# A hybrid decoder layer on one core: the output projection's turned rows copied out of PSUM first, four summed pairs in its second block, and weight buffers dealt by kind

## The chip, the core and the metric

The kernel runs on one core of one Trainium2 chip. The metric is the device time of one execution in microseconds (us). The median of three runs of the kernel before is 1082.09 us (1081.95 to 1083.99).

The engines are named as in the profile: PE is the matrix engine (PEld its weight loads), DVE the vector engine, ACT the scalar engine, POOL GpSimd, SP the engine that issues most of the loads.

## The reference

One decoder layer on 256 tokens of width 2048, in float32:

```python
u = rmsnorm(h, ln1_w)
lru_x, lru_g, q, k, v, ret_g = split(u @ w_in)        # six parts of 1024
y_lru = rg_lru(conv4(lru_x)) * gelu(lru_g)            # group A
y_ret = groupnorm(retention(rope(q), rope(k), v)) * silu(ret_g)   # group B, 8 heads
h = h + concat(y_lru, y_ret) @ w_out                  # 2048 x 2048
u = rmsnorm(h, ln2_w)
h = h + (silu(u @ w_gate) * (u @ w_up)) @ w_down      # D_FF = 5632
return rmsnorm(h, final_norm_w)
```

## The kernel before

**Split products.** Every float32 operand of a large product is cut into a high and a low part of a shorter matmul format: `split` (L122 to L124) is an ACT cast into `wh` (`ah`, `sh`, `bh`, `t4h`) and a DVE subtraction into `wl` (`al`, `sl`, `bl`, `t4l`). A product is then three matmuls, high by high, high by low and low by high (`three`, L683 to L685, tile `c`). Loads of weights bring 128x1024 raw tiles (512 KB) from SP's queue; each is cast by ACT, subtracted by DVE, and read by PE.

**Stages.** First v, the eight tiles of lru_x, k and q, v and the gates, each with its scan or its retention; then the output projection in two blocks of 1024 columns (block 0 and block 1, here "output blocks"), then the FFN's blocks 2 to 12, the down projection (two blocks) and the final norm. On the time axis, output block 0's steps run from about 294 to 343 us and block 1's to about 388.

**Pairs and steps.** A block's contraction of 2048 is cut into eight pairs of 256. A *plain* pair takes the eight half products of `EIGHT`, 24 matmuls of 128x512 in all, and two loads. A *summed* pair takes seven products (`SEVEN`, a Strassen-like scheme), 21 matmuls, but three loads, and sums of weights (`add`, L661, four DVE additions of 128x512) and of the left operand (`Left`, L561 to L564, four DVE additions of 128x128) that must be split as well. Its work comes in two parts: `share` (letter `s`, 12 matmuls: p1, p5, p6, p7), run in the steps of the block *before*, and `direct` (letter `d`, 9 matmuls), run in its own block. `STEPS` gives each block's sequence of letters (`p` plain, `h` half a plain pair), `SUMMED` says which pairs of a block are summed. In the kernel before block 0 has none, and block 1 has two (pairs 4 and 5).

**Turning rows.** When all of an output block's columns for both token tiles are complete, `post` (L594 to L603) adds the residual (DVE, L597, `htok`), squares it for the next norm (ACT, L598, `junk`) and writes it to memory (ACT's queue, L599). `turn(p)` (L581 to L592) then makes the FFN's left operand: four PE transposes (L588) into a PSUM tile `ht`, two ACT copies out of it with the norm's weight (L591, `hf`), and at once `Left(f, ...)`, the split and, for summed pairs, the sums. The turns run within the first plain step of the next block, after its fourth product (`plain`, `n == 4`).

**The first norm.** `squares` (L305 to L311) lets ACT square the eight tiles of x, the first into `sumsq`, and POOL adds the other seven to it; PE then sums over partitions with the matmul `rms` (L271).

**Order and buffers.** The program is written as a list of steps; a tile scheduler orders the instructions of each engine by their place in it and by its own estimate of time, and inserts the waits. Raw tiles come from a pool of 6 buffers, splits from a pool of 4; from block 3 to block 11 each has two buffers more, dealt out in turn (every fourth raw tile, every third split).

Of the kernel before, what the change touches and what calls it, by code (L numbers as in the profile page):

```python
# [30 lines left out]

SUMMED = ((), (4, 5), (2, 3), (1, 2, 3)) + ((0, 1, 2, 3),) * 8 + ((1, 2, 3),)
SUMMED_OUT, SUMMED_FFN = (4, 5), (0, 1, 2, 3)

PLAIN = ((4, 5, 6, 7, 0, 1, 2, 3),) * 2 + (tuple(range(8)),) * 11
STEPS = ("pppspppspp", "ppspdpsdpp", "pdpsdpspspp", "pspsdpsdpsdp") + ("psdhsdhsdhsdhp",) * 7 + ("psdpsdpsddp", "psdpsdpsdpp")


EARLY_DOWN = (0, 1, 2)
# [5 lines left out]
def tile_hymba_layer(ctx: ExitStack, tc: tile.TileContext, A: dict, out: bass.AP):  # L45
# [4 lines left out]
    apool = ctx.enter_context(tc.tile_pool(name="acts", bufs=60))  # L50
    rpool = ctx.enter_context(tc.tile_pool(name="raw", bufs=6))
    wpool = ctx.enter_context(tc.tile_pool(name="split", bufs=4))
# [3 lines left out]
    tpool = early.enter_context(tc.tile_pool(name="tmp", bufs=6))  # L56
    late, resid, more, turn_of = [], [xpool], [], [0, 0]
    extra = ExitStack()
# [15 lines left out]
    def split_tiles():  # L74
        turn_of[1] += 1
        pool_ = more[1] if more and turn_of[1] % 3 == 0 else wpool
        return [pool_.tile([P, 1024], F32R, tag=g, name=nm(g)) for g in ("wh", "wl")]

    def raw_tile():
        turn_of[0] += 1  # L80
        pool_ = more[0] if more and turn_of[0] % 4 == 0 else rpool
        return pool_.tile([P, 1024], F32, tag="raw", name=nm("raw"))
# [207 lines left out]
    r2_tok = cpool.tile([P, 2], F32, name="r2_tok")  # L290
    sumsq = cpool.tile([P, 512], F32, name="sumsq")

# [146 lines left out]
    trig = [None]  # L439
    cr = cpool.tile([P, S], F32, name="cr")  # L440
    sr = cpool.tile([P, S], F32, name="sr")
    decay = [None] * NH
# [104 lines left out]
    class Left:  # L547
# [21 lines left out]
        def __getitem__(self, which):  # L569
            n = self.names.index(which)  # L570
            o = n % 4 * P
            return self.h[n // 4][:, o : o + P], self.l[n // 4][:, o : o + P]

    sq2 = cpool.tile([P, 2, 4], F32, name="sq2")
    v2 = cpool.tile([P, 2], F32, name="v2")
# [4 lines left out]
    def out_post(d):  # L580


        def turn(p):
            pt, f = room(d)("ht"), act_tile("hf")
            for c in range(2):
                for t in range(2):
                    h = htok[p // 2, t][:, (p % 2) * S + c * P : (p % 2) * S + c * P + P]
                    pe.transpose(pt[:, c * S + t * P : c * S + t * P + P], h, ident)  # L588
            for c in range(2):
                cs = slice(c * S, c * S + S)  # L590
                act.activation(out=f[:, cs], in_=pt[:, cs], func=AF.Copy, scale=col(C_LN2 + 2 * p + c))  # L591
            hh[p] = Left(f, p in SUMMED_FFN)  # L592

        def post(c, ps):  # L594
# [5 lines left out]
            if t:  # L600
                turns.extend(lambda p=p: turn(p) for p in (2 * cb, 2 * cb + 1))
            if (cb, t) == (3, 1):
                v.tensor_reduce(out=v2, in_=sq2, axis=mybir.AxisListType.X, op=ALU.add)  # L603
# [13 lines left out]
    class Quad:  # L617
# [5 lines left out]
        def __init__(self, src, sums, before=None):  # L623
            self.src, self.sums, self.before = src, sums, before
            self.parts = {}
            self.apart = False

# [11 lines left out]
        def load(self, half):  # L639
            r = raw_tile()  # L640
            nc.sync.dma_start(out=r, in_=self.src[:, half * 1024 : half * 1024 + 1024])
# [118 lines left out]
    class Direct(Quad):  # L760
# [8 lines left out]
        def load(self, half):  # L769
            r = raw_tile()  # L770
            nc.sync.dma_start(out=r, in_=self.src[:, 1024:2048])
# [14 lines left out]
    class Block:  # L786
# [45 lines left out]
        def put(self, after):  # L832
            plain = [i for i in PLAIN[self.index] if i not in self.summed]
            for k, kind in enumerate(self.steps):
                if kind == "p":
                    i, n = plain.pop(0), len(plain)
                    quad = Quad(self.src(i), False)
                    run = lambda i=i, quad=quad, k=k, n=n: self.plain(i, quad, k == 0, n == 0)
                elif kind == "h":
# [408 lines left out]
```

## Time and profile before

| | us |
|---|---|
| median of three runs | 1082.09 |
| the profiled execution | 1082.46 |
| its span, first to last instruction | 1080.7 |
| PE busy | 1070.2 (99%) |
| PE weight loads busy | 897.7 (83%) |
| DVE busy | 964.1 (89%) |
| ACT busy | 664.5 (61%) |
| POOL busy | 57.2 (5%) |

Busy times are sums of the profiler's records and stand beside the span of the one profiled execution. The 1.8 us between that execution's time and its span lie before the first and after the last instruction. Matmuls are pipelined, so the duration of one row is longer than its distance to the next; distances are read from start times.

### The profile page before, as it was taken

What the parts mean: (1) busy time and instruction counts of PE and PEld (TensorE: products, weight loads), DVE (VectorE), ACT (ScalarE), POOL (GpSimd) and SP (SyncE); (2) the same over time, 40 slices, a digit from 0 to 9 for tenths busy, and PEclk for the clock granted to TensorE, in tenths of its full rate; (3) what the DMA queues carried; (4) which work ended last, traced back from release to release, by engine and by line L of the source; (5) the groups of instructions that cost most, each with busy time, mean ns of one, the idle gap of its engine ahead of it and who ended that gap; (6) DMA issues with size and microseconds to landing.
All of it is one profiled execution on the core that took longest, in us unless ns stands there. A gap on an engine that the chain in (4) does not pass through costs nothing.

```text
span 1080.7 us, 14590 instructions
## 1 busy us (share of the span) xinstructions
PE 1070.2 (99%) x5089; PEld 897.7 (83%) x5089; DVE 964.1 (89%) x1399; ACT 664.5 (61%) x947; POOL 57.2 (5%) x73
## 2 busy tenths in 40 slices
PE   9999999999999999999999999999999999999997
PEld 7888888888888888888888888888888888888886
DVE  7889789988878889989999999999999889997886
ACT  7666644468756676656656565665656656654563
POOL 0602230000000000000000000000002000000001
PEclk9999999999999999999999999999999999999999
DMA  9965475554556588677776777777767856474662
GB/s 325 336 213 171 159 254 166 183 176 158 192 195 234 183 304 273 231 235 256 257 270 228 251 260 242 263 269 232 258 234 270 289 181 214 162 245 159 214 212 101
DMA packets 71386, 244.62 MB, mean 226 GB/s; under 512 B 8208, under 2 KB 8592, under 8 KB 71312
## 3 DMA queue, kind: packets, MB, share of 16 engines
q1 hardware_dynamic: 68400, 236.34, 64.6%
q0 software_dynamic: 1472, 4.72, 1.3%
q10 hardware_dynamic: 1440, 2.62, 0.6%
q8 instruction: 40, 0.66, 0.2%
q14 instruction: 34, 0.28, 0.1%
HBM read 239.46 MB, written 4.19 MB: 225 GB/s over the span
## 4 chain that ended last, share of the span: by engine, by line
PE 98%; DVE 1%; DMA 1%; POOL 0%; SPq 0%; ACT 0%; issue 0%; POOLq 0%; ACTq 0%
PE c L685 22%; PE c L683 22%; PE c L684 22%; PE fm L194 11%; PE fm L196 5%; PE tm L174 3%; PE tm L175 3%; PE tm L176 3%; PE p L683 1%; PE p L685 1%; PE p L684 1%; PE ft L865 1%; DMA x<-in_x 1%; PE ht L588 0%; PE sc L492 0%; DVE wl L124 0%
## 5 line engine op out<-in xcount | busy, mean ns | idle before, releaser
L123 ACT CAST wh<-raw 128x1024 fp32r<-128x1024 f32 (+1 forms) x498 | 462.9, 959 | 323.8 <-PE c L685 130.8
L124 DVE TENSOR_TENSOR wl<-raw,wh 128x1024 fp32r<-128x1024 f32 (+1 forms) x498 | 542.2, 1115 | 72.5 <-ACT wh L123 71.2
L684 PE MATMUL c<-wl,ah 128*128 128x512 f32 x826 | 322.7, 391 | 0.0
L685 PE MATMUL c<-wh,al 128*128 128x512 f32 x826 | 321.8, 390 | 0.0
L683 PE MATMUL c<-wh,ah 128*128 128x512 f32 x826 | 280.3, 391 | 0.0
L683 PEld LDWEIGHTS c<-wh,ah 128*128 128x128 f32 x826 | 155.1, 188 | 32.0 <-ACT wh L123 0.3
L685 PEld LDWEIGHTS c<-wh,al 128*128 128x128 f32 x826 | 155.2, 188 | 31.8
L684 PEld LDWEIGHTS c<-wl,ah 128*128 128x128 f32 x826 | 155.2, 188 | 31.6
L194 PE MATMUL fm<-u,wh 128*128 128x512 f32 x512 | 161.4, 396 | 0.0
L196 PEld LDWEIGHTS fm<-u,wl 128*128 128x128 f32 x512 | 96.1, 188 | 22.4
L196 PE MATMUL fm<-u,wl 128*128 128x256 f32 x512 | 101.2, 279 | 0.0
L661 DVE TENSOR_TENSOR raw<-raw,raw 128x512 f32<-128x512 f32 x114 | 78.4, 689 | 2.0
L661 DVE TENSOR_TENSOR raw<-raw 128x512 f32<-128x512 f32 x114 | 78.3, 688 | 1.4
L194 PEld LDWEIGHTS fm<-u,wh 128*128 128x128 f32 x512 | 78.4, 189 | 0.3
L684 PE MATMUL c<-wl,sh 128*128 128x512 f32 x192 | 74.3, 390 | 0.0
L685 PE MATMUL c<-wh,sl 128*128 128x512 f32 x192 | 73.7, 390 | 0.0
L683 PE MATMUL c<-wh,sh 128*128 128x512 f32 x192 | 67.3, 391 | 0.3 <-ACT sh L123 0.3
L176 PE MATMUL tm<-wh,u 128*128 128x512 f32 x128 | 48.7, 391 | 0.0
L175 PE MATMUL tm<-wl,u 128*128 128x512 f32 x128 | 48.7, 393 | 0.0
L174 PE MATMUL tm<-wh,u 128*128 128x512 f32 x128 | 46.9, 394 | 1.4 <-ACT u L298 1.4
L683 PEld LDWEIGHTS c<-wh,sh 128*128 128x128 f32 x192 | 36.1, 188 | 8.1 <-ACT sh L123 0.7
L685 PEld LDWEIGHTS c<-wh,sl 128*128 128x128 f32 x192 | 36.1, 188 | 7.5
(247 smaller groups left out, 1027.4 us busy)
## 6 DMA issues: line engine op xcount, KB each, us to landing
raw<-in_w_gu SPq DMA_DIRECT2D x216, 512.0 KB, 5.3
raw<-in_w_down SPq DMA_DIRECT2D x91, 512.0 KB, 4.6
raw<-in_w_out SPq DMA_DIRECT2D x34, 512.0 KB, 3.7
raw<-in_w_lx SPq DMA_DIRECT2D x16, 512.0 KB, 6.4
raw<-in_w_k SPq DMA_DIRECT2D x16, 512.0 KB, 3.6
raw<-in_w_q SPq DMA_DIRECT2D x16, 512.0 KB, 4.2
raw<-in_w_rg SPq DMA_DIRECT2D x16, 512.0 KB, 3.5
raw<-in_w_lg SPq DMA_DIRECT2D x16, 512.0 KB, 3.5
```

Source lines behind the costliest of these rows:

```text
L123: act.copy(out=dst_h, in_=src)
L124: v.tensor_tensor(out=dst_l, in0=src, in1=dst_h.bitcast(F32), op=ALU.subtract)
L174: pe.matmul(ps, ah, wh, start=first, stop=False)
L175: pe.matmul(ps, ah, wl, start=False, stop=False)
L176: pe.matmul(ps, al, wh, start=False, stop=last)
L194: pe.matmul(ps, wh, hl, start=n + i == 0, stop=False)
L196: pe.matmul(ps[:, :S], wl, hl[:, :S], start=False, stop=n + i == len(order) - 1)
L661: v.tensor_tensor(out=dst, in0=a, in1=b, op=ALU.add)
L683: pe.matmul(p, ah, bh, start=first, stop=False, skip_group_check=onto)
L684: pe.matmul(p, ah, bl, start=False, stop=False, skip_group_check=onto)
L685: pe.matmul(p, al, bh, start=False, stop=last, skip_group_check=onto)
L865: pe.transpose(pt[:, o : o + P], g[:, (2 * b + c) * P : (2 * b + c) * P + P], ident)
```

## The change

It has four parts.

1. Block 1 sums four pairs (4 to 7) instead of two. Block 0's steps take four shares instead of two, and block 1's take four `d` instead of two; `SUMMED_OUT` has the left operands of these pairs summed as well.
2. `turn` now ends with the copies out of PSUM (into `flipped[p]`); the splits, `left(p)`, are deferred each by a number of steps of its own, in the table `LEFTS`.
3. The raw pool has 7 buffers instead of 6. The two extra ones of the FFN are given by kind instead of in turn: to the second loads of `Direct` and of a block's last plain pair (`brief`).
4. `sumsq` moves from the constants' pool to an act tile; the rotary tables `cr` and `sr` become the halves of one act tile `turned`.

```diff
-SUMMED = ((), (4, 5), (2, 3), (1, 2, 3)) + ((0, 1, 2, 3),) * 8 + ((1, 2, 3),)
-SUMMED_OUT, SUMMED_FFN = (4, 5), (0, 1, 2, 3)
+SUMMED = ((), (4, 5, 6, 7), (2, 3), (1, 2, 3)) + ((0, 1, 2, 3),) * 8 + ((1, 2, 3),)
+SUMMED_OUT, SUMMED_FFN = (4, 5, 6, 7), (0, 1, 2, 3)
-STEPS = ("pppspppspp", "ppspdpsdpp", "pdpsdpspspp", "pspsdpsdpsdp") + ...
+STEPS = ("ppspspspsppp", "psdpsdpddp", "pdpsdpspspp", "pspsdpsdpsdp") + ...
+LEFTS = ((2, 1), (3, 2), (0, 4), (1, 6)), ((4, 1), (5, 1), (6, 2), (7, 3))
-    rpool = ctx.enter_context(tc.tile_pool(name="raw", bufs=6))
+    rpool = ctx.enter_context(tc.tile_pool(name="raw", bufs=7))
-    def raw_tile():
-        turn_of[0] += 1
-        pool_ = more[0] if more and turn_of[0] % 4 == 0 else rpool
+    def raw_tile(brief=False):
+        pool_ = more[0] if more and brief else rpool
-    sumsq = cpool.tile([P, 512], F32, name="sumsq")
+    sumsq = act_tile("sumsq")
-    cr = cpool.tile([P, S], F32, name="cr")
-    sr = cpool.tile([P, S], F32, name="sr")
+    turned = act_tile("turned")
+    cr, sr = turned[:, :S], turned[:, S:]
...
                 act.activation(out=f[:, cs], in_=pt[:, cs], func=AF.Copy, scale=col(C_LN2 + 2 * p + c))
-            hh[p] = Left(f, p in SUMMED_FFN)
+            flipped[p] = f
+
+        def left(p):
+            hh[p] = Left(flipped[p], p in SUMMED_FFN)
...
                 turns.extend(lambda p=p: turn(p) for p in (2 * cb, 2 * cb + 1))
+                if cb % 2:
+                    turns.append(lambda: [defer(n, lambda p=p: left(p)) for p, n in LEFTS[d]])
...
-            self.apart = False
+            self.apart = self.brief = False
...
-            r = raw_tile()
+            r = raw_tile(self.brief and half == 1)
...
     class Direct(Quad):
...
-            r = raw_tile()
+            r = raw_tile(True)
...
                     quad = Quad(self.src(i), False)
+                    quad.brief = n == 0
```

Instructions before and after: 128x512 matmuls 4265 and 4259; on DVE 24 more (8 raw sums, 8 sums of left operands, 4 splits of half weight tiles, 2 of `t4`, 2 of left sums); on ACT 8 more casts of 128x512; on SP 2 more loads of w_out.

How the order changes at three places; numbers behind a name tell tiles apart, line numbers in rows of the change are the changed file's.

PE in the first stage, where the matmul `rms` takes in the sum of squares; `fm` is a tile of lru_x. Before:

```order
L196 MATMUL fm_526<-u_263,wl_471 128x256
L194 MATMUL fm_526<-u_298,wh_470 128x512
L271 MATMUL rms_543<-ones,sumsq 128x2 x2
L194 MATMUL fm_526<-u_303,wh_470 128x512
L196 MATMUL fm_526<-u_298,wl_471 128x256
L196 MATMUL fm_526<-u_303,wl_471 128x256
```

and in the change:

```order
L197 MATMUL fm_525<-u_262,wl_470 128x256
L272 MATMUL rms_542<-ones,sumsq_111 128x2 x2
L195 MATMUL fm_525<-u_297,wh_469 128x512
L195 MATMUL fm_525<-u_302,wh_469 128x512
L197 MATMUL fm_525<-u_297,wl_470 128x256
L197 MATMUL fm_525<-u_302,wl_470 128x256
```

The `rms` matmuls stand one matmul earlier. On ACT the square of the first tile, which stood near the start between the casts for v, now follows the last weight cast before it and the two copies of v, just ahead of the other squares:

```order
L124 CAST wh_342<-raw_341 128x1024
L1044 COPY v_359<-tm_207 128x512
L1044 COPY v_373<-tm_208 128x512
L309 ACTIVATE sumsq_111<-x_82 128x512
L309 ACTIVATE sq_377<-x_83 128x512
L309 ACTIVATE sq_380<-x_84 128x512
```

The chain of POOL's additions thus starts after one more square.

ACT at the boundary of block 0 and block 1; `junk` is the square of an output row, DMA its way to memory, `hf` a copy out of PSUM (x2: two of them), `wh` and `t4h` casts of weights, `ah` the cast of a left operand, `sh` that of its sums. Before:

```order
L598 ACTIVATE junk_3621,sq_119<-htok_2982 128x512
L599 DMA kept_rows<-htok_2982 128x512
L123 CAST wh_3632<-raw_3630 128x512
L591 ACTIVATE hf_3649<-ht_3648,small 128x256 x2
L123 CAST ah_3656<-hf_3649 128x512
L123 CAST wh_3752<-raw_3630 128x1024
L123 CAST wh_3632<-raw_3744 128x512
L123 CAST sh_3665<-s_3660 128x512
L591 ACTIVATE hf_3670<-ht_3669,small 128x256 x2
L123 CAST wh_3762<-raw_3760 128x1024
L123 CAST ah_3677<-hf_3670 128x512
```

and in the change:

```order
L124 CAST wh_3717<-raw_3663 128x1024
L124 CAST wh_3727<-raw_3725 128x1024
L124 CAST wh_3665<-raw_3709 128x512
L124 CAST t4h_3721<-raw_3709 128x512
L593 ACTIVATE hf_3744<-ht_3743,small 128x256 x2
L593 ACTIVATE hf_3752<-ht_3751,small 128x256 x2
L593 ACTIVATE hf_3760<-ht_3759,small 128x256 x2
L593 ACTIVATE hf_3768<-ht_3767,small 128x256 x2
L124 CAST wh_3802<-raw_3800 128x1024
L124 CAST ah_3787<-hf_3760 128x512
L124 CAST wh_3808<-raw_3806 128x1024
L124 CAST wh_3843<-raw_3841 128x512
```

The copies, which came two at a time with casts between them, now stand eight in a row, ahead of the cast of `wh_3802`.

DVE right behind that, in the change; `wl_3844` and `raw_3841` belong to a pair that is shared in block 1, `s_3832` are the sums of the second of block 0's turned rows to be split:

```order
L565 TENSOR_TENSOR s_3791<-hf_3760,s_3791 128x128
L125 TENSOR_TENSOR wl_3844<-raw_3841,wh_3843 128x512
L125 TENSOR_TENSOR sl_3797<-s_3791,sh_3796 128x512
L668 TENSOR_TENSOR raw_3841<-raw_3841 128x512
L125 TENSOR_TENSOR al_3829<-hf_3768,ah_3828 128x512
L562 TENSOR_TENSOR s_3832<-hf_3768 128x128
L564 TENSOR_TENSOR s_3832<-hf_3768 128x128
L668 TENSOR_TENSOR raw_3841<-raw_3841,raw_3856 128x512
L563 TENSOR_TENSOR s_3832<-hf_3768,s_3832 128x128
L668 TENSOR_TENSOR raw_3856<-raw_3841,raw_3856 128x512
L565 TENSOR_TENSOR s_3832<-hf_3768,s_3832 128x128
L668 TENSOR_TENSOR raw_3856<-raw_3856 128x512
```

Between the splits of weights stand the sums of two left operands, four rows each, and the four raw sums of a shared pair; `sh` on ACT needs the last `s_3832`.

## Rows read from the trace of the kernel before

**Rows 1.** The page, chain that ended last, by engine.
```profile
PE 98%; DVE 1%; DMA 1%; POOL 0%; SPq 0%; ACT 0%; issue 0%; POOLq 0%; ACTq 0%
```

**Rows 2.** Waits of PE: engine, line waited for, total us, times, longest.
```profile
PE tm L174 <- ACT u L298: 1.4, 2, 1.0
...
PE c L683 <- ACT sh L123: 0.3, 1, 0.3
```

**Rows 3.** PE timeline in block 0: start us, us, instruction.
```profile
299.66 0.39 PE L685 MATMUL c<-wh,al 128*128 128x512 f32 x1
...
308.50 0.39 PE L685 MATMUL c<-wh,al 128*128 128x512 f32 x1
```

**Rows 4.** Stretches: busy us (instructions) of PE, PEld, DVE, ACT, POOL, PEclk, DMA share, GB/s.
```profile
260.00:294.00 34.00, 34.00 (x198) 29.67 (x197) 30.91 (x61) 28.34 (x51) 0.00 (x0) 1.00 0.56 186
300.00:340.00 40.00, 40.00 (x178) 33.11 (x177) 30.78 (x38) 20.11 (x26) 0.00 (x0) 1.00 0.64 218
310.00:320.00 10.00, 10.00 (x46) 8.29 (x45) 5.72 (x6) 4.84 (x5) 0.00 (x0) 1.00 0.84 282
340.00:380.00 40.00, 39.70 (x183) 32.53 (x182) 35.71 (x56) 28.34 (x45) 0.00 (x0) 1.00 0.60 200
370.00:380.00 10.00, 9.70 (x43) 7.52 (x42) 10.00 (x12) 8.03 (x11) 0.00 (x0) 1.00 0.75 247
500.00:600.00 100.00, 100.00 (x451) 82.97 (x450) 95.16 (x120) 60.43 (x79) 0.00 (x0) 1.00 0.76 255
```

**Rows 5.** PE timeline around the late wait.
```profile
370.40 0.50 PE L683 MATMUL c<-wh,ah 128*128 128x512 f32 x1
...
371.77 0.39 PE L684 MATMUL c<-wl,sh 128*128 128x512 f32 x1
```

**Rows 6.** ACT timeline there; brackets: idle before, releaser.
```profile
368.34 2.52 ACT L123 CAST wh<-raw 128x1024 fp32r<-128x1024 f32 x3 [1.82 <-DVE raw L661]
370.77 0.61 ACT L123 CAST sh<-s 128x512 fp32r<-128x512 f32 x1
```

**Rows 7.** ACT timeline, start of the second stage.
```profile
28.79 1.06 ACT L1036 COPY v<-tm 128x512 f32<-128x512 f32 x2
29.74 3.76 ACT L308 ACTIVATE sq<-x 128x512 f32<-128x512 f32 x7
```

**Rows 8.** POOL timeline, the same stage.
```profile
30.47 12.58 POOL L310 TENSOR_TENSOR sumsq<-sumsq,sq 128x512 f32<-128x512 f32 x7 [29.59 <-ACT sq L308]
43.13 1.60 POOL L311 TENSOR_TENSOR sumsq<-sumsq 128x256 f32<-128x256 f32 x1
```

**Rows 9.** PE timeline at the sum of squares.
```profile
44.85 0.40 PE L194 MATMUL fm<-u,wh 128*128 128x512 f32 x1
45.08 0.50 PE L271 MATMUL rms<-ones,sumsq 128*128 128x2 f32 x4
```

**Rows 10.** DVE timeline, fourth output addition of block 0.
```profile
340.88 0.69 DVE L597 TENSOR_TENSOR htok<-c,htok 128x512 f32<-128x512 f32 x1 [0.38 <-PE c L685]
```

**Rows 11.** PE timeline, end of block 0 and the transposes.
```profile
340.46 0.39 PE L685 MATMUL c<-wh,al 128*128 128x512 f32 x1
...
344.21 1.80 PE L588 MATMUL ht<-ident,htok 128*128 128x128 f32 x15
```

**Rows 12.** ACT by form, 200 to 440 us: busy, mean ns | idle before, releaser.
```profile
L123 ACT CAST wh<-raw 128x1024 fp32r<-128x1024 f32 x82 | 85.7, 1051 | 60.8 <-PE c L685 19.3 <-DVE raw L661 13.2 <-PE tm L176 12.7
...
L591 ACT ACTIVATE hf<-ht,small 128x256 f32<-128x256 f32 x16 | 6.7, 467 | 0.4 <-PE ht L588 0.4
```

**Rows 13.** DVE by form, the same stretch.
```profile
L124 DVE TENSOR_TENSOR wl<-raw,wh 128x1024 fp32r<-128x1024 f32 x84 | 102.0, 1221 | 19.8 <-ACT wh L123 19.4
...
L661 DVE TENSOR_TENSOR raw<-raw 128x512 f32<-128x512 f32 x16 | 11.0, 689 | 0.3
```

**Rows 14.** DVE timeline, small sums of a left operand.
```profile
347.01 0.28 DVE L561 TENSOR_TENSOR s<-hf 128x128 f32<-128x128 f32 x1
347.21 0.29 DVE L563 TENSOR_TENSOR s<-hf 128x128 f32<-128x128 f32 x1
```

More of the change, by code (lines that the diff above doesn't have):

```diff
@@ L28 @@
 N_SMALL = 104
-SUMMED = ((), (4, 5), (2, 3), (1, 2, 3)) + ((0, 1, 2, 3),) * 8 + ((1, 2, 3),)
-SUMMED_OUT, SUMMED_FFN = (4, 5), (0, 1, 2, 3)
+SUMMED = ((), (4, 5, 6, 7), (2, 3), (1, 2, 3)) + ((0, 1, 2, 3),) * 8 + ((1, 2, 3),)
+SUMMED_OUT, SUMMED_FFN = (4, 5, 6, 7), (0, 1, 2, 3)
 PLAIN = ((4, 5, 6, 7, 0, 1, 2, 3),) * 2 + (tuple(range(8)),) * 11
-STEPS = ("pppspppspp", "ppspdpsdpp", "pdpsdpspspp", "pspsdpsdpsdp") + ("psdhsdhsdhsdhp",) * 7 + ("psdpsdpsddp", "psdpsdpsdpp")
+STEPS = ("ppspspspsppp", "psdpsdpddp", "pdpsdpspspp", "pspsdpsdpsdp") + ("psdhsdhsdhsdhp",) * 7 + ("psdpsdpsddp", "psdpsdpsdpp")
+LEFTS = ((2, 1), (3, 2), (0, 4), (1, 6)), ((4, 1), (5, 1), (6, 2), (7, 3))
 EARLY_DOWN = (0, 1, 2)
@@ L56, in tile_hymba_layer @@
     tpool = early.enter_context(tc.tile_pool(name="tmp", bufs=6))
-    late, resid, more, turn_of = [], [xpool], [], [0, 0]
+    late, resid, more, turn_of = [], [xpool], [], [0]
     extra = ExitStack()
@@ L74, in split_tiles @@
     def split_tiles():
-        turn_of[1] += 1
-        pool_ = more[1] if more and turn_of[1] % 3 == 0 else wpool
+        turn_of[0] += 1
+        pool_ = more[1] if more and turn_of[0] % 3 == 0 else wpool
         return [pool_.tile([P, 1024], F32R, tag=g, name=nm(g)) for g in ("wh", "wl")]
-    def raw_tile():
-        turn_of[0] += 1
-        pool_ = more[0] if more and turn_of[0] % 4 == 0 else rpool
+    def raw_tile(brief=False):
+        pool_ = more[0] if more and brief else rpool
         return pool_.tile([P, 1024], F32, tag="raw", name=nm("raw"))
@@ L572, in __getitem__ @@
             return self.h[n // 4][:, o : o + P], self.l[n // 4][:, o : o + P]
+    flipped = {}
     sq2 = cpool.tile([P, 2, 4], F32, name="sq2")
```

## The prediction

> **What bounds the kernel now.** I read the chain of waits first: TensorE (PE) carries 98% of the path that ended last [rows 1]. Then the waits of PE: once its first data were there it waited three times, twice on ScalarE's `u` (1.4 us, in the first projection) and once on ScalarE's split `sh` [rows 2]. So the time is the number of matmuls times their spacing, plus the few places where PE is held up. The spacing: in PE's timeline from the matmul at 299.66 to the one at 308.50 there are 39 steps, 8.84/39 = 0.2267 us each [rows 3]; the rows' 0.39 us each overlap and are not the price. The granted clock is 1.00 in every stretch of the table by stretches, so no clock term enters [rows 4]. A faster VectorE (DVE) or ScalarE (ACT) is worth nothing by itself; a slower one costs only from the moment PE has to wait.
>
> The one late wait lies in output block 1. Between the matmuls that start at 370.40 and 371.77 three spacings took 1.37 us instead of 0.68: 0.69 lost [rows 5]. ACT shows why: its casts there had waited 1.82 us for DVE's raw sums, and `sh`, started at 370.77, came last [rows 6]. DVE is the engine behind: busy 10.00 of 10 us from 370 to 380 [rows 4].
>
> **The change part by part.** The sum is made against the profiled execution's own time, 1082.46 us; the median of the runs shown, 1082.09, is 0.37 below it.
>
> *A, fewer matmuls.* Two more of block 1's pairs are summed: 21 matmuls instead of 24 each, six fewer of 128x512. 6 x 0.2267 = **-1.36**.
>
> *B, the wait at 370 us.* In the new order this pair's first part runs in block 0 (its shares sit between plain pairs), and all copies out of PSUM are ahead of the casts. The `sh` that was late then is not at that place any more: **-0.69**. If it returns there, 0.
>
> *C, the sum of squares at the start.* `sumsq` leaves the constants' pool for an act tile, and ACT forms its first square not early but directly after the two copies of `v`, ahead of the seven others. Before, these copies started at 28.79 and the squares at 29.74, seven in 3.76 us, which is 0.52 from one to the next without the last one's overlap of 0.1 [rows 7]; GpSimd (POOL), which adds them, started at 30.47 and ended at 44.73 [rows 8]. PE's `rms` matmul came at 45.08, one matmul after the one of 44.85, with no wait [rows 9]. Now the chain starts one square later, 0.52, ending at 45.25, and the order puts `rms` one matmul earlier on PE, with its turn at 44.85. A weight load of about 0.1 ahead of that makes the wait up to 0.75. One raw buffer more lets a weight load of this stage start sooner, which may bring the copies and with them the squares forward; the lower bound holds that. I take **+0.6**, nearest to the row of the squares; bounds 0 and +0.8.
>
> *D, the boundary of the two blocks.* Let T be the end of block 0's fourth output addition on DVE; before, it was 340.88 + 0.69 = 341.57 [rows 10], 1.11 after the start of that output's last matmul at 340.46 [rows 11]. By the new order PE passes 33 matmuls and 16 transposes (0.11 each: fifteen took 1.80 with 0.27 for the last [rows 11]) between that matmul and the first use of the weights `wh_3802`: T - 1.11 + 0.23 + 33 x 0.2267 + 16 x 0.11 = T + 8.4.
> ACT reaches these weights thus. Back to back, each instruction costs its duration less the 0.08 to 0.1 by which neighbours overlap: casts of 128x1024 0.95, of 128x512 0.52, copies out of PSUM 0.37 [rows 6, 12]; on DVE 1.14, 0.60 and, for a 128x128 sum, 0.20 [rows 13, 14]. DVE first splits half a tile and adds two raw sums (T + 2.0). Then ACT: two casts of 1024, two of 512, **eight copies in a row** (2.9), then the cast of `wh_3802` (1.05): T + 2.0 + 1.9 + 1.05 + 2.9 + 1.05 = T + 8.9. With 0.1 for the weight load ahead of the matmul, PE waits about 0.6. Before, the copies came two at a time, each pair behind other casts.
> DVE has stood idle for that cast, and then has 18 instructions up to the raw sum that the cast ahead of `sh_3837` needs, two splits of 1024, eight halves and eight small sums: 2 x 1.14 + 8 x 0.60 + 8 x 0.20 = 8.7, T + 17.6. ACT's half cast and `sh_3837` itself, 0.6 each, bring it to T + 18.8. PE wants it 42 matmuls after `wh_3802`: T + 8.4 + 9.5 = T + 17.9, and 0.6 later for the wait it has had, T + 18.5; with 0.1 for the load a wait of about 0.5. Together **+1.1**. Bounds: 0 and 2.5, some twice the sum, since each wait is the difference of two chains of 9 and 18 us, and 5% in either of the chains removes it or doubles it.
>
> *E, at nothing.* DVE gets 24 more instructions: 16 halves (8 raw sums, 4 and 2 splits of weights, 2 of left operands) and 8 small sums, 16 x 0.60 + 8 x 0.20 = 11.2 us. ACT gets 8 half casts, 4.2 us. The cover: from 300 to 380 DVE was busy 30.78 + 35.71 of 80 us, 13.5 idle, and ACT 31.6 idle [rows 4]. 2.8 us of the eleven (the sums and splits of two left operands) fall before 294, where DVE was idle 3.1 of 34 us [rows 4]. Two loads more on SP and the renamed raw buffers: DMA's share was 0.60 to 0.64 in these stretches [rows 4], and PE never waited for a load there [rows 2]. In the FFN seven raw buffers and two extra for the short-lived halves take the place of six and two in turn: a ninth lets loads start earlier, and since no wait of PE names one, that is worth nothing; nor do I see a loss, as the halves that get the extra two are split and free again at once. From block 2 on the steps are as before. Cover gone, the price is the second rival's.
>
> *PSUM banks.* The transposed halves used to lie in PSUM till they were split; now all four are copied out at once. In the rows PE never waits for a bank: its one late wait names ACT's split [rows 2], so I price it at 0. What ACT's rows do price is the queue of copies, the 2.9 us in D. The Trainium skill, PSUM — Partial Sum Buffer, Summary: rules for kernel authors, asks to evacuate PSUM promptly; by it copying ahead is a gain, and the sum without D, the first rival's time.
>
> **Sum:** -1.36 - 0.69 + 0.6 + 1.1 = -0.35, so 1082.1 for a profiled execution, **1081.7 us** on the scale of the median.
>
> **The rivals.**
> *First: the new waits stay hidden.* Both waits of D are differences of long chains, and a lead of 0.6 us more for the splits at T removes them. Then -1.36 - 0.69 = -2.05, with C between 0 and 0.6: 1080.0 to 1080.6. For it: in all of the trace PE lost only 0.69 after the first projection [rows 2, 5]. Against: DVE and ACT start from T at the same distance as before, with more ahead of the same matmuls.
> *Second, slower: DVE becomes the bound of the output blocks.* Between the fourth output addition of block 0 and that of block 1 the new listing gives DVE 15 splits of 1024, 29 halves and 15 small sums: 17.1 + 17.4 + 3.0 = 37.5 us [rows 13, 14], and PE 156 x 0.2267 + 16 x 0.11 = 37.1 us. To this comes DVE's idling for `wh_3802`, some 2.4 us (its nine instructions from T on, 2 x 1.14 + 7 x 0.60, take 6.5 of the 8.9): DVE falls 2.8 us back in this block, and can only live on splits made ahead. In the FFN that follows it is busy 95.16 of 100 us [rows 4], so what it owes at the end is paid at the next tight pair. If it all is paid, and block 0's 4.3 us without work between 310 and 320 [rows 4] find no load to use, the waits are 4.3 instead of 1.1: -2.05 + 0.6 + 4.3 = +2.85, 1084.9. It decides from 3.6 us of waits on. Against: the six matmuls fewer are taken from block 1 while the DVE work of the shares moves to block 0, which gets 54.4 us of matmuls instead of 49.0.
> *Third: the change does less than it says.* The wait B is a late DVE; with more DVE work it may come back unchanged beside D. -0.35 + 0.69 = +0.34: 1082.4, inside the range of the forecast.
>
> **The numbers.** About 0.2%, 2.16 us, is what a measurement of this kernel can tell from no change: 1079.9 to 1084.3 is "same". The forecast 0.45 and the third rival 0.12, together 1080.7 to 1083.3 and all of it the same: 0.57. First rival 0.25: its 1080.0 lies at the edge, and with the scatter of the runs somewhat more than half of it ends beyond 1079.9: 0.15. Second rival 0.18, nearly all of it slower. Faster 0.15, same 0.67, slower 0.18. The range: it must reach into both rivals, down to A and B in full with C at nothing and a little for the scatter of the runs, 1079.7, and up to the second rival's price, 1084.9.
>
> **What would show it.** A: 4259 matmuls of 128x512. B: no wait of PE on `sh` late in block 1, where the one of 370 us stood. C: a wait of PE at `rms` of 0.4 to 0.8, released by POOL. D: two waits of PE near T + 8 and T + 18, the first on a split of weights, the second on `sh`, and eight `hf` copies in one row on ACT ahead of the first. Wrong it would be if PE's waits from 300 us to 450 us sum to over 3.5 us (DVE near 10 of 10 through block 1: the second rival), or if there are none (the first).

## The result, and the profile after

The change is slower: 1086.57 us median (1086.4 to 1087.3, five runs) beside 1082.41 for the kernel before; the ratio is 1.0038, interval 1.0027 to 1.0049. That is 4.2 us, above the range's end of 1084.9, where 1081.7 was forecast. The profiled execution took 1087.3 us with a span of 1085.5, 4.8 more than before, at a granted clock of 0.998 as before.

PE's waits after, in total us, times and longest:

```profile
PE c L690 <- ACT wh L124: 2.9, 7, 0.7
...
PE tm L175 <- ACT u L299: 0.8, 1, 0.8
```

Against [rows 2] the wait on `sh` at 370 us is gone (term B), and seven waits on casts of weights stand in its place. The places of most of them, in PE's timeline; the first four rows are term D:

```profile
354.99 0.39 PE L692 MATMUL c<-wh,sl 128*128 128x512 f32 x1
355.95 0.97 PE L690 MATMUL c<-wh,ah 128*128 128x512 f32 x3 [0.57 <-ACT wh L124]
...
365.40 0.39 PE L692 MATMUL c<-wh,al 128*128 128x512 f32 x1
365.89 0.98 PE L690 MATMUL c<-wh,sh 128*128 128x512 f32 x3
```

From 354.99 to 355.95 is 0.96 us where a step is 0.23 [rows 3]; with the slow step behind it, 0.84 us are lost, and at 365.40 another 0.38. Then come waits in block 2 and, from 438 us on, at the start of block 3, where nothing was expected:

```profile
410.02 0.39 PE L692 MATMUL c<-wh,al 128*128 128x512 f32 x1
410.93 0.73 PE L690 MATMUL c<-wh,sh 128*128 128x512 f32 x2 [0.52 <-ACT wh L124]
411.88 0.50 PE L690 MATMUL c<-wh,ah 128*128 128x512 f32 x1 [0.22 <-ACT wh L124]
...
439.31 0.60 PE L873 MATMUL ft<-ident,gated 128*128 128x128 f32 x4
440.62 0.49 PE L690 MATMUL c<-wh,sh 128*128 128x512 f32 x1 [0.71 <-ACT wh L124]
441.57 0.73 PE L690 MATMUL c<-wh,ah 128*128 128x512 f32 x2 [0.45 <-ACT wh L124]
```

The matmul at 410.93 starts 0.91 us after the one ahead of it, that at 440.62 has waited 0.71 us and that at 441.57 another 0.45; in all some 3.0 us are lost at these two places. The rest: 0.6 us at 840, 0.9 at 949, 0.6 between 1010 and 1045. The excess of PE's steps over the normal step (the usual distance between two matmuls of these shapes), summed by stretch, gives this account of the two profiled executions:

| stretch, us | before | after | difference |
|---|---|---|---|
| 0 to 60 | 2.38 | 2.16 | -0.2 |
| 345 to 378 (boundary of the output blocks, and the old wait at 370) | 0.79 | 1.40 | +0.6 |
| 400 to 445 (block 2, start of block 3) | 0.18 | 3.42 | +3.2 |
| 830 to 1050 (last FFN block, down projection) | 0.18 | 2.18 | +2.0 |
| six matmuls fewer | | | -1.4 |

That makes +4.2; the last matmul ends 4.7 us later. Matched matmul by matmul, the change falls back by 3.4 us between 398 and 445, by 0.6 at 840, 0.9 at 949 and 0.7 between 1010 and 1050: most of what the table lacks lies around the same waits, in steps too little longer to be counted in it.

Where the time began to go, on ACT at the first boundary, with the end of the fourth output addition on DVE (T = 346.14 + 0.69 = 346.83) ahead of it:

```profile
346.14 0.69 DVE L602 TENSOR_TENSOR htok<-c,htok 128x512 f32<-128x512 f32 x1 [0.67 <-PE c L692]
```

```profile
349.00 2.52 ACT L124 CAST wh<-raw 128x1024 fp32r<-128x1024 f32 x3 [1.41 <-DVE raw L668]
351.42 0.62 ACT L124 CAST t4h<-raw 128x512 fp32r<-128x512 f32 x1
351.94 3.03 ACT L593 ACTIVATE hf<-ht,small 128x256 f32<-128x256 f32 x8
354.81 1.09 ACT L124 CAST wh<-raw 128x1024 fp32r<-128x1024 f32 x1
...
363.75 1.57 ACT L124 CAST wh<-raw 128x1024 fp32r<-128x1024 f32 x2 [2.60 <-DVE raw L668]
365.22 0.62 ACT L124 CAST sh<-s 128x512 fp32r<-128x512 f32 x1
```

The cast behind the eight copies ends at 355.90, T + 9.1; the forecast had T + 8.9. `sh` ends at 365.84, T + 19.0; the forecast had T + 18.8. And by stretches (columns as in [rows 4]):

```profile
300.00:340.00 40.00, 40.00 (x178) 33.15 (x177) 38.39 (x48) 24.07 (x31) 0.00 (x0) 1.00 0.72 245
340.00:380.00 40.00, 39.32 (x180) 32.02 (x180) 34.14 (x52) 27.17 (x45) 0.00 (x0) 1.00 0.68 234
380.00:390.00 10.00, 10.00 (x47) 8.24 (x46) 10.00 (x17) 4.27 (x6) 0.00 (x0) 1.00 0.83 279
390.00:400.00 10.00, 10.00 (x54) 8.43 (x53) 6.25 (x13) 9.97 (x23) 0.00 (x0) 1.00 0.79 275
```

DVE's holes of [rows 4] were used: 38.39 of 40 us busy between 300 and 340 instead of 30.78. From 380 to 390 DVE is full (10.00). From 390 to 400 ACT is full (9.97) and DVE, waiting for it, does only 6.25 us of work. Before, ACT was nearly as full there, and DVE did 7.84:

```profile
390.00:400.00 10.00, 10.00 (x53) 8.43 (x52) 7.84 (x15) 9.81 (x19) 0.00 (x0) 1.00 0.80 292
```

### The profile page after: what moved, and what is told of

It is laid out like the page before. It is cut to its first block, busy times and chain, and to the rows that moved or that the text cites. A ratio compares the mean times of both kernels' runs of the same rounds, so it can differ in the third digit from the quotient of the medians.

```text
span 1085.5 us, 14632 instructions
## 1 busy us (share of the span) xinstructions
PE 1072.5 (99%) x5083; PEld 895.5 (82%) x5083; DVE 974.5 (90%) x1423; ACT 667.4 (61%) x955; POOL 55.8 (5%) x73
## 4 chain that ended last, share of the span: by engine, by line
PE 92%; DVE 2%; POOL 1%; issue 1%; DMA 1%; ACT 1%; SPq 0%; POOLq 0%; ACTq 0%
PE c L690 22%; PE c L691 22%; PE c L692 22%; PE fm L195 10%; PE fm L197 5%; PE tm L176 2%; PE tm L175 2%; PE tm L177 2%; POOL sumsq L311 1%; PE p L691 1%; PE p L692 1%; PE p L690 1%; PE ft L873 1%; DMA raw<-in_w_lx 1%; DVE wl L125 1%
## 5 line engine op out<-in xcount | busy, mean ns | idle before, releaser
L691 PE MATMUL c<-wl,ah 128*128 128x512 f32 x814 | 317.4, 390 | 0.0
L692 PE MATMUL c<-wh,al 128*128 128x512 f32 x814 | 316.6, 390 | 0.0
L690 PE MATMUL c<-wh,ah 128*128 128x512 f32 x814 | 275.4, 392 | 1.7 <-ACT wh L124 1.7
L690 PEld LDWEIGHTS c<-wh,ah 128*128 128x128 f32 x814 | 152.1, 188 | 36.1 <-ACT wh L124 5.4
L668 DVE TENSOR_TENSOR raw<-raw,raw 128x512 f32<-128x512 f32 x118 | 81.0, 687 | 2.3 <-DMA raw<-in_w_down 0.3
L668 DVE TENSOR_TENSOR raw<-raw 128x512 f32<-128x512 f32 x118 | 81.0, 687 | 1.6
L691 PE MATMUL c<-wl,sh 128*128 128x512 f32 x200 | 77.6, 389 | 0.0
L692 PE MATMUL c<-wh,sl 128*128 128x512 f32 x200 | 77.1, 389 | 0.0
L690 PE MATMUL c<-wh,sh 128*128 128x512 f32 x200 | 70.6, 393 | 1.3 <-ACT wh L124 1.2
L691 PEld LDWEIGHTS c<-wl,sh 128*128 128x128 f32 x200 | 37.5, 188 | 7.8
```

What stands on the lines that cost most here:

```text
L668: v.tensor_tensor(out=dst, in0=a, in1=b, op=ALU.add)
L690: pe.matmul(p, ah, bh, start=first, stop=False, skip_group_check=onto)
L691: pe.matmul(p, ah, bl, start=False, stop=False, skip_group_check=onto)
L692: pe.matmul(p, al, bh, start=False, stop=last, skip_group_check=onto)
```

## The experiments

Three parts can be taken apart: **pairs** (four summed pairs and the steps), **turns** (copies first, splits by the table) and **pools** (seven raw buffers, the extra ones by kind, sum of squares and tables in act tiles). Theories: *arrears* (DVE has too much to do, the second rival), *burst* (ACT is full at the boundaries and DVE idles behind it), *kinds* and *deal* (other tiles get the extra buffers). Ratios are to the kernel before on the same chip.

**Pairs alone.** The kernel before with

```diff
-SUMMED = ((), (4, 5), ...
+SUMMED = ((), (4, 5, 6, 7), ...
-STEPS = ("pppspppspp", "ppspdpsdpp", ...
+STEPS = ("ppspspspsppp", "psdpsdpddp", ...
```

> The kernel before with only the four summed pairs and the new steps; turns, pools and the sum of squares as before. Theory 'arrears' (the 11 us more of DVE work use up the splits made ahead, and PE waits in blocks 1 and 2 whatever the order of the turns): about 3 us of waits between 345 and 445 us, 1084 to 1086 us. Theory 'burst' (the copies out of PSUM, eight in a row, hold up the casts and with them DVE): no waits but one near the old place, 1.36 us of matmuls gone, 1080.5 to 1082 us. Neither expects waits of PE after 800 us.

Measured: 1092.5 us, 1.009 (1.0073 to 1.0107), worse than either theory said. One wait does most of it. PE's timeline, then two stretches:

```profile
361.23 0.39 PE L685 MATMUL c<-t4h,al 128*128 128x512 f32 x1
365.94 0.79 PE L683 MATMUL c<-wh,ah 128*128 128x512 f32 x1 [4.32 <-ACT ah L123]
...
371.24 0.63 PE L683 MATMUL c<-wh,sh 128*128 128x512 f32 x1
371.67 0.63 PE L684 MATMUL c<-wl,sh 128*128 128x512 f32 x1
```

```profile
360.00:370.00 10.00, 4.89 (x15) 2.99 (x14) 8.56 (x19) 5.98 (x11) 0.00 (x0) 0.71 0.28 99
370.00:380.00 10.00, 10.00 (x36) 8.08 (x35) 6.90 (x12) 6.17 (x8) 0.00 (x0) 0.78 0.41 129
```

PE stood from 361.23 to 365.94 for a left operand, `ah`: the rows are turned and split in the order 0, 1, 2, 3, and the first share now needs the third of them, with two splits and their sums ahead of it. Behind the stall the granted clock is 0.71 and 0.78 in the two stretches, and the matmuls from 366.5 to 374 mostly stand 0.427 us apart, which is 512 columns at the lower of the clock's two levels, 1.2 GHz: some 3.5 us more. A second wait among them, at 366.95 for `sh`, takes another 1.1. The Trainium skill, TensorE: Matmul & The Clock Gate, Why this matters for your kernels, warns that idle gaps of PE bring the low clock back; the rows agree. In the change, whose longest step is 1 us, every stretch up to 1070 us has 1.00. Of the waits from 400 to 445 only 0.3 us, at 446, is there, but PE comes to it late, so the run does not tell whether the pairs alone would bring them.

**Turns alone.** Old pairs, steps and pools, with `flipped`, `left` and `LEFTS`.

> The kernel before with only the turns changed (all copies first, splits deferred by the table); two summed pairs, old steps, old pools. Theory 'burst': ACT casts come 2 to 3 us later at both boundaries of output blocks, DVE stands idle meanwhile, and PE waits for 2 to 3 us in all between 345 and 445 us: 1084 to 1085.5 us. Theory 'arrears': DVE has no more work than before and makes up for it, waits within 0.5 us of before, 1082 to 1083 us.

Measured: 1082.15 us, 0.9994 (0.9985 to 1.0003). The profile lists no wait of PE after the first projection, not even that of 370 us. So the burst costs nothing where the first share comes a plain pair later (steps `pps...` instead of `ps...`). Nor does it at the second boundary, the end of block 1, though the squares, the table load and eight copies in a row (391.02 to 394.04) stand on ACT there too: no `sh` waits ahead of them, and DVE is not full:

```profile
380.00:390.00 10.00, 10.00 (x50) 8.34 (x49) 8.30 (x13) 6.86 (x14) 0.00 (x0) 1.00 0.88 311
```

**Pools alone.**

```diff
-    rpool = ctx.enter_context(tc.tile_pool(name="raw", bufs=6))
+    rpool = ctx.enter_context(tc.tile_pool(name="raw", bufs=7))
...
-        pool_ = more[0] if more and turn_of[0] % 4 == 0 else rpool
+        pool_ = more[0] if more and brief else rpool
...
-    sumsq = cpool.tile([P, 512], F32, name="sumsq")
+    sumsq = act_tile("sumsq")
...
```

> The kernel before with only the buffers changed (seven raw buffers, the two extra by kind, sum of squares and rotary tables in act tiles). Theory 'kinds' (the extra raw buffers, given by kind, delay loads or raw sums in the late FFN and the down projection): the waits of PE after 830 us that the change shows, 2.0 us in all, appear here too, and the start is 0.2 to 0.5 us shorter: 1083.5 to 1084.5 us. Otherwise: no waits after 830 us, 1081.5 to 1082.5 us.

Measured: 1083.67 us, 1.0011 (1.0002 to 1.002). In the profile 0.8 us of waits stand between 1010 and 1045 us and 0.3 at the sum of squares; the waits at 840 and 949 are not there. Half a miss for *kinds*. The run does not part the seventh raw buffer, the deal by kind and the act tiles; the extra buffers end with block 11, ahead of this stretch, and the seventh stays.

**All but the pools.** The change with the buffers of before.

> The change with the buffers of before (six raw, two extra in turn, sum of squares and tables in the constants' pool). Theory 'kinds': the waits after 830 us are gone and block 2 waits as in the change, 1084.5 to 1085 us. If the late waits come from the order that the scheduler gives to the whole program: they stay, 1086 to 1087 us. If the seventh buffer helped blocks 1 and 2: more waits there, over 1087 us.

Measured: 1087.43 us, 1.0043 (1.0028 to 1.0057). The waits at 840 and 949 stay, 0.6 and 0.9 us, and one of 1.2 us is new at 523; those between 1010 and 1045 are gone. So the first two belong to the pairs, though the pairs' work ended 450 us earlier, and the last group to the pools: each of the nine profiles with the new buffers has it, 0.1 to 2.5 us; of the seven without, two have 0.4 and 0.7 us between 998 and 1011 (turns, and the last kernel with copies on DVE), the others nothing. Block 2's waits are here as in the change, 3.0 us between 400 and 445, so pairs and turns together are enough for them.

How can two pairs in block 1 be felt in block 12? `split_tiles` counts: every third split in the FFN takes an extra buffer. A summed pair makes three splits through it where a plain one makes two, so two pairs more hand the extra buffers to other tiles. (In the buffers of before every fourth raw tile is counted too, and two loads more shift that. The wait at 523 stands in both runs with the pairs on these buffers, at 528 in pairs alone, and not in the last kernel below, with both counters set.)

**The counter alone.**

```diff
-    late, resid, more, turn_of = [], [xpool], [], [0]
+    late, resid, more, turn_of = [], [xpool], [], [1]
```

> The change with the counter of the split buffers started at 1 instead of 0. Every third split in the FFN gets one of two extra buffers, counted from the program's first split; the two new summed pairs add two splits ahead of the FFN and so shift which tiles get them. Theory 'deal': with the old tiles dealt the extra buffers, the waits of PE near 840 and 949 us (0.5 and 0.8 us in the change, the same in the runs with pairs and without pools, absent without the pairs) are gone, 1085.0 to 1085.5 us. Theory 'arrears' (DVE still owes work from blocks 1 and 2): they stay, 1086.3 to 1087 us.

Measured: 1084.85 us, 1.0017 (1.0008 to 1.0026) against the change's 1.0038. The waits at 840 and 949 are gone, and, not foreseen, that at 440 (1.7 us) with them; between 1010 and 1045 us it has 1.1 us instead of 0.6. What a deal does is seen on ACT in block 12, in the change first, with the counter at 1 below:

```profile
832.30 0.62 ACT L124 CAST wh<-raw 128x512 fp32r<-128x512 f32 x1
836.59 0.62 ACT L124 CAST sh<-s 128x512 fp32r<-128x512 f32 x1 [3.66 <-DVE s L565]
837.26 3.47 ACT L124 CAST wh<-raw 128x1024 fp32r<-128x1024 f32 x4
```

```profile
829.23 1.57 ACT L124 CAST wh<-raw 128x1024 fp32r<-128x1024 f32 x2 [1.71 <-PE c L692]
831.78 0.62 ACT L124 CAST sh<-s 128x512 fp32r<-128x512 f32 x1 [0.97 <-DVE s L565]
834.39 3.47 ACT L124 CAST wh<-raw 128x1024 fp32r<-128x1024 f32 x4 [1.99 <-DVE raw L668]
```

The order of casts is another one, and the counter is all that differs: in the change half a tile goes ahead and `sh` then holds the queue for 3.66 us, with the four casts that PE wants behind it; with the counter at 1 two casts go ahead of `sh`, which waits 0.97. Block 12 itself is dealt no extra buffers, which end with block 11; by what way the deal before it changes the order there is not shown.

The converse, the **kernel before with the counter shifted** and nothing else:

```diff
-    late, resid, more, turn_of = [], [xpool], [], [0, 0]
+    late, resid, more, turn_of = [], [xpool], [], [0, 2]
```

> The kernel before with nothing changed but the counter of the split buffers, started at 2: the same shift of every third split as the change's two summed pairs bring. Theory 'deal': the waits near 840 and 949 us appear in it (0.5 and 0.8 us) and perhaps one in block 2 or 3, 1083.5 to 1085 us. If the shift needs the new pairs to hurt: as before, 1082 to 1083 us.

Measured: 1084.03 us, 1.0008 (0.9998 to 1.0017). The profile has 0.9 us of waits at 946 and 0.2 at 837: the deal hurts without the pairs, by less than in the change, and the ratio alone would not tell it.

**Squares and root later.** In `post`, the square, the reduction and the reciprocal root go through `defer(6, ...)`:

```diff
-            act.activation(out=act_tile("junk"), in_=h, func=AF.Square, accum_out=sq2[:, t, cb : cb + 1])
+            defer(
+                6,
+                lambda: act.activation(
+                    out=act_tile("junk"), in_=h, func=AF.Square, accum_out=sq2[:, t, cb : cb + 1]
+                ),
+            )
...
-                v.tensor_reduce(out=v2, in_=sq2, axis=mybir.AxisListType.X, op=ALU.add)
-                rsqrt_small(r2_tok, v2, 1.0 / D, 2)
+                defer(6, lambda: v.tensor_reduce(out=v2, in_=sq2, axis=mybir.AxisListType.X, op=ALU.add))
+                defer(6, lambda: rsqrt_small(r2_tok, v2, 1.0 / D, 2))
```

> The change with the squares of the output rows and the reciprocal root that follows them deferred by six steps, so that 4 squares, a table load and the root no longer stand with the eight copies at the two boundaries. Theory 'burst' (ACT is full at the boundary of blocks 1 and 2, DVE idles for it 3.7 of 10 us, and PE pays at 410 and 440 us): the 3.0 us of waits there fall below 1, 1083.5 to 1085 us. Theory 'arrears' (DVE simply has more work than PE leaves time for): within 0.5 us of the change, 1086 to 1087 us.

Measured: 1085.61 us, 1.0023 (1.0013 to 1.0033); the excess between 400 and 445 falls from 3.4 to 0.5 us. ACT at the second boundary in the change, and then the stretches from 380 to 400 with the squares later:

```profile
388.80 0.62 ACT L124 CAST sh<-s 128x512 fp32r<-128x512 f32 x1 [3.07 <-DVE s L565]
...
393.82 3.00 ACT L593 ACTIVATE hf<-ht,small 128x256 f32<-128x256 f32 x8
396.85 1.28 ACT L259 ACT_TABLE_LOAD   x1
```

```profile
380.00:390.00 10.00, 10.00 (x50) 8.37 (x49) 9.97 (x17) 6.98 (x14) 0.00 (x0) 1.00 0.79 275
390.00:400.00 10.00, 10.00 (x50) 8.28 (x49) 9.04 (x13) 9.06 (x18) 0.00 (x0) 1.00 0.64 234
```

In the change `sh` waits 3.07 us for a sum of DVE, the four squares wait behind it, then the eight copies, then the table load; DVE then waits for ACT's squares, root and casts, and does 6.25 of 10 us. With squares, table load and root out of the way it does 9.04, after being as full from 380 to 390 as in the change (9.97). Which of the three does it, no run parts.

**Less work for DVE.** The change without the sums:

```diff
-            self.add(r)
+            if self.summing:
+                self.add(r)
```

`summing` is false for the shares of block 1 alone.

> The change without the 16 raw sums of weights of block 1's four summed pairs: t1 to t4 are formed from the weights as loaded. DVE has 9.6 us less to do between 295 and 385 us, all else is left. Theory 'arrears': the 4.3 us of waits between 345 and 445 us fall below 1, 1082.5 to 1083.5 us. Theory 'burst': the wait at the first boundary shrinks at most by the two sums ahead of the casts, that of block 2 stays, 1085.5 to 1086.5 us.

Measured: 1087.2 us, 1.0037 (1.0024 to 1.005): nothing gained. By stretches, and at the first wait:

```profile
300.00:340.00 40.00, 40.00 (x179) 33.10 (x178) 28.79 (x32) 23.08 (x29) 0.00 (x0) 1.00 0.76 257
390.00:400.00 10.00, 10.00 (x53) 8.42 (x52) 6.30 (x12) 9.97 (x23) 0.00 (x0) 1.00 0.73 262
```

```profile
354.70 0.39 PE L692 MATMUL c<-wh,sl 128*128 128x512 f32 x1
355.66 1.20 PE L690 MATMUL c<-wh,ah 128*128 128x512 f32 x4 [0.57 <-ACT wh L124]
```

DVE has 9.6 us less to do in block 0 (28.79 instead of 38.39), and PE's step at the first wait is 0.96 us as in the change, 0.73 of it lost. From 390 to 400 DVE does 6.30 us, as in the change. *Arrears* has fallen for block 0: no debt is carried out of it. For block 1 the run before this one speaks: with the squares later DVE has as much to do as in the change, and the waits of block 2 are gone. So a full DVE does not make them by itself; the order of ACT's queue must add to it. That DVE's late sum is their first link stays likely: it is what `sh` waits for in the change, and no run takes work from DVE in block 1.

**Counter and squares together.**

> Both edits in one: counter at 1 and squares deferred. If each does its part alone (deal and burst): 1082 to 1083.5 us, as fast as the kernel before. If neither does: 1086 to 1087 us.

Measured: 1083.34 us, 1.0003 (0.9994 to 1.0012), as the two theories' sum said: the kernel before's time within the interval. Left in the profile are the first boundary's 1.2 us and 1.7 us near 1018, of the pools' group.

**Copies shared with DVE.** In `turn`, for `c == 1`:

```diff
+                if c:
+                    v.tensor_scalar(
+                        out=f[:, cs], in0=pt[:, cs], scalar1=col(C_LN2 + 2 * p + c), scalar2=None, op0=ALU.mult
+                    )
+                    continue
```

> The change with every second copy out of the transposes' PSUM tiles made by DVE, which stood idle 2.1 us there, instead of ACT: four copies in a row on ACT and four on DVE. Theory 'burst' for the first boundary (eight copies ahead of the cast of weights make PE wait at 355 and 365 us, 0.84 and 0.38 us): the first wait goes, the second shrinks, and block 2's wait at 410 us shrinks too, since ACT is full at that boundary: 1084 to 1085.5 us. If these waits hang on the transposes or the weights' loads instead: the waits stay, 1086 to 1087 us.

Measured: 1087.39 us, 1.0037 (1.0025 to 1.005). A miss. On ACT, and on PE:

```profile
351.87 1.56 ACT L598 ACTIVATE hf<-ht,small 128x256 f32<-128x256 f32 x4
353.35 1.05 ACT L124 CAST wh<-raw 128x1024 fp32r<-128x1024 f32 x1
355.35 1.05 ACT L124 CAST wh<-raw 128x1024 fp32r<-128x1024 f32 x1 [0.94 <-PE c L697]
356.30 0.61 ACT L124 CAST ah<-hf 128x512 fp32r<-128x512 f32 x1
```

```profile
355.15 1.07 PE L695 MATMUL c<-wh,ah 128*128 128x512 f32 x4
356.97 0.50 PE L695 MATMUL c<-wh,ah 128*128 128x512 f32 x1 [0.75 <-ACT ah L124]
```

The cast behind the copies came 1.5 us earlier, and the wait at 354.99 is gone. But the next cast of weights, which waits 0.94 us for PE to release a buffer, now stands ahead of the left operand `ah`, and PE waits 0.9 us for that. A wait for a buffer at the head of ACT's queue holds up what is ready behind it. The Trainium skill, PSUM — Partial Sum Buffer, Engine vs sequencer instructions, says that ScalarE's queue is strictly first in, first out; the two rows agree. The waits of block 2 did not shrink either: 3.3 us of excess between 400 and 445.

**All repairs, and a later share.** Counter, squares and copies on DVE; then counter and squares with block 1's steps `ppsdpsdddp`.

> All three repairs on the change: counter at 1, squares deferred, every second copy on DVE. The 1.2 us of waits at the first boundary that counter and squares left go or halve, so about 1 us less than with those two alone: 0.999 of the kernel before, 1081.5 to 1082.5 us. If the copies on DVE only move the wait (DVE late with its sums): 1083 us or more.

> Counter at 1, squares deferred, and block 1's first share moved one plain pair later (steps ppsdpsdddp instead of psdpsdpddp), copies as in the change. Theory 'burst': the left operands have 5.4 us more before a share needs them, the wait at 365 us goes, the one at 355 (a plain pair's weights behind the copies) may stay: 1082 to 1083 us. If the three direct parts in a row at the end leave DVE too little time: new waits near 380 us, 1084 us or more.

Measured: 1083.36 us, 0.9999 (0.999 to 1.0008), and 1084.82 us, 1.0017 (1.0008 to 1.0026). The copies moved the first boundary's wait (1.4 us stay), and the later share removed it (0.2 us of excess left between 345 and 378) but paid 1.7 us at 378 to 381, where the direct parts now stand three in a row; 0.5 us at 412 and 2.5 between 1020 and 1044 (1.8 with counter and squares alone) come with it. So the first boundary's wait depends on the steps; this other sequence only moved its price.

**Everything aligned.** The four pairs and the turns on the old buffers, with both counters set so that the FFN's tiles get the buffers of before, and squares later:

```diff
-    late, resid, more, turn_of = [], [xpool], [], [0, 0]
+    late, resid, more, turn_of = [], [xpool], [], [2, 1]
```

> The four pairs and the new turns on the buffers of before (six raw, sum of squares in the constants), both counters started so that the FFN's tiles get the extra buffers as before (raw at 2, splits at 1), squares and root deferred by six steps. If deal, kinds and the squares are all that the change lost beside the first boundary's 1.2 us: no waits after 400 us beyond those of the kernel before, 6 matmuls fewer, the wait at 370 us gone, so -1.36 - 0.69 + 1.2 = -0.85 us, a ratio of 0.999. If the order of the whole program breaks anyway: a ratio of 1.001 or more, with waits at other places.

> The same with every second copy on DVE. In the two runs that had this, the first wait (355 us) was not removed but passed to the cast of a left operand: so 355 and 365 us stay at 1.2 to 1.4 us, and block 2 as in the run without it: a ratio of 0.999 as well. If ACT's relief at the second boundary counts: 0.998.

> The kernel of aligned once more, for a profile of an undisturbed execution. If the parts named are the whole loss: PE waits at 355 and 365 us (1.2 us together) and nowhere else after 60 us, none at 410, 440, 523, 840, 949 or 1010 to 1045 us; a ratio of 0.999 again.

Measured: 1082.14 us, 0.999 (0.9981 to 0.9999), and in the second run 1081.91 us, 0.9992 (0.9983 to 1.0001); with copies on DVE 1083.05 us, 0.9999 (0.9991 to 1.0008), where 0.3 us at 410 and 0.7 near 1000 stand beside the first boundary's 1.4. PE's waits in the second run of the first of these, and DVE from 390 to 400:

```profile
PE tm L176 <- ACT u L300: 1.3, 2, 0.9
...
PE c L696 <- ACT wh L125: 0.6, 1, 0.6
```

```profile
390.00:400.00 10.00, 10.00 (x50) 8.28 (x49) 9.03 (x13) 8.98 (x18) 0.00 (x0) 1.00 0.67 254
```

After the first projection PE's waits are those at 355 and 365 us (the second is too short for the list of waits), 1.2 us together; no other place has more than 0.1 beyond the kernel before. The sum for it, -1.36 - 0.69 + 1.2 = -0.85, came out at -0.95 and -0.78 us between medians. It has the lowest ratio of the study, by about as much as can be told from no change: the second interval reaches 1.0001, and turns alone (0.9994) is not told from it.

## Why the prediction was wrong

**A and B held.** 4259 matmuls, and the wait of 370 us is gone.

**C was half right.** The start of the squares moved as described, and the chain of POOL with it:

```profile
30.29 13.11 POOL L311 TENSOR_TENSOR sumsq<-sumsq,sq 128x512 f32<-128x512 f32 x7 [29.42 <-ACT sq L309]
43.48 1.07 POOL L312 TENSOR_TENSOR sumsq<-sumsq 128x256 f32<-128x256 f32 x1
```

```profile
44.12 0.39 PE L197 MATMUL fm<-u,wl 128*128 128x256 f32 x2
44.60 0.61 PE L272 MATMUL rms<-ones,sumsq 128*128 128x2 f32 x4
45.07 0.71 PE L195 MATMUL fm<-u,wh 128*128 128x512 f32 x2
```

It ended at 44.55 instead of the forecast's 45.25, since the copies of `v` came 0.7 us earlier, at 28.09 instead of 28.79 [rows 7]; that the seven additions took 13.11 us instead of 12.58 and the last one 1.07 instead of 1.60 [rows 8] cancels. Matched matmul by matmul, PE lost 0.34 at `rms`, where 0.6 was taken, after gaining 0.50 in the first projection, which no term had. (By the forecast's own terms the wait was 45.25 + 0.1 - 44.85 = 0.5; its 0.75 does not follow from them.)

**D held in place and size.** 1.22 us measured beside 1.1 forecast, at T + 8.2 and T + 18.6, the first on a cast, not yet on its split, the second on `sh`. ACT's chains of 9 and 18 us were each right to 0.2 us. (The second wait, by its own terms, is 18.8 - 18.5 + 0.1 = 0.4, not 0.5.)

**E is the step that failed**: "From block 2 on the steps are as before", and the whole of its cover at nothing. Two things were read wrongly in it.

- The second boundary was not worked out. The reckoning that gave D was made for block 0's end alone, but at the end of block 1 eight copies come again, with four squares, a table load and a root. In the change `sh` stands ahead of them and waits 3.07 us for a DVE that is full, so all of them come late; turns alone has these instructions there without that `sh`, with DVE at 8.30 of 10, and no wait follows. The later squares and the counter show its price: 3.4 us of excess between 400 and 445, of which 3.0 go with the squares, and the 1.7 at 440 also with the counter. Either repair nearly removes the wait at 440 (0.4 is left with the squares later).
- "Steps as before" is not "buffers as before". A pool that deals its extra buffers by counting hands them to other tiles when two splits are added ahead of it, and the casts come in another order as far as block 12 and the down projection: 1.4 us at 840 and 949, gone with the counter at 1. The new buffers, priced at nothing "since no wait of PE names one", added 0.6 between 1010 and 1045; by what way, and which of them, is not shown, only that this group comes and goes with them. That no wait named these buffers before held for the order of before alone.

**The second rival had the sign, and its mechanism at most in part.** DVE was not the bound of block 0: with 9.6 us taken off it there nothing changed, and the hole between 310 and 320, whose loss it feared, was filled (9.86 of 10 us). Its price, 4.3 us of waits, is near what was measured between 345 and 445 (1.2 + 3.0) by chance, as the debt it was made of was not there. Of the sign that was set for it, over 3.5 us of waits with DVE near 10 of 10 through block 1, the waits came, but DVE did 34.14 of 40 us from 340 to 380 and was full only from 380 to 390. There its late sum takes part in the price. That "what it owes at the end is paid at the next tight pair" whatever ACT does is refuted: with DVE as full and another order on ACT, block 2 waits for nothing.

**On PSUM** the price of 0 held: turns alone is the same as before within its interval, and in no run's list of waits does PE wait for a bank there. What the new turns are worth depends on the steps: with the new ones, pairs alone is 1.009 and pairs with turns 1.0043, where the wait for `ah` is gone. With `LEFTS` the left operand that the first share needs is split first; whether that or the copying ahead does it, no run parts.

## What to carry to other kernels

When a schedule is shifted at one place, work out every place where the same pattern recurs, and look in the program for what counts or takes turns: a buffer dealt by a counter ties distant stages together. On an engine that takes its instructions in order, a new one is priced by what stands behind it when it waits. And a stage in which nothing waits says that its order fits its buffers, not that buffers don't matter there.

## What was not expected of the hardware

One stall of 4.3 us on PE (pairs alone) cost about 3.5 us more in slow matmuls behind it, 0.427 instead of 0.227 us apart for 8 us; the stalls of the change, 1 us at most, left the granted clock at 1.00. POOL's last addition of 256 columns took 1.60 us before and 1.07 in the change, with the same shape, and its seven additions of 512 columns 12.58 and 13.11. The seven are not alike: before, the first three took 1.29 to 1.31 us each, and the next three, from 34.59 us on, when DVE's splits run beside them, 2.16 to 2.27; of those splits of 128x1024 the ones that started at 35.62 and 37.87 took 2.31 to 2.32 us where 1.22 is usual [rows 13].
